# A two-layer FoX and NSA decoder on one Trainium2 core: the end of w_up in 256 columns, weight sums by accumulating transfers, the first output half behind the products, compressed scores by two heads

## The chip, the cores and the metric

The kernel runs on one core of one Trainium2 chip. Its engines are named here as the profile names them: PE is the matrix engine (PEld its weight loads), DVE is VectorE, ACT is ScalarE, POOL is GpSimd, and SP only issues transfers. Each engine works through its own instructions in a fixed order; a transfer is issued by SP, ACT or POOL and then runs by itself. The metric is the time of one execution on the device, in microseconds (us), as the median of several runs.

## The reference

A trunk of two layers on x of 512 tokens by 1024 channels, all in float32, with a final RMSNorm. Per layer:

```python
h = rmsnorm(x, norm_mix)
proj = h @ w_in                      # q, k, v, gates of both mixers
o_a = fox_attention(...)             # 8 heads of 64, softmax(q k / 8 + c_i - c_j), causal
o_c, o_s, o_w = nsa_attention(...)   # 8 heads, 2 key heads: compressed, selected, window
o_n = g[..., 0:1] * o_c + g[..., 1:2] * o_s + g[..., 2:3] * o_w
mixed = sigmoid(gate_a) * (o_a @ w_o_fox) + sigmoid(gate_b) * (o_n @ w_o_nsa)
x = x + mixed @ w_out
h = rmsnorm(x, norm_mlp)
x = x + square(relu(h @ w_up)) @ w_down      # 1024 -> 4096 -> 1024
```

The compressed branch scores each query against 31 compressed keys per key head (blocks of 32 tokens, stride 16); four query heads share a key head. The MLP is the larger half of the work.

## The kernel before

Everything is kept transposed: channels on the 128 partitions, the 512 tokens along the free axis. Every float32 product is made of three reduced-precision products: a value is split into a high part (`h`, a copy to float32r) and a low part (`lo`, the rest), and `h*xh + h*xl + lo*xh` is summed in PSUM (`gemm`, L243 to L245). So each weight block costs one cast on ACT and one subtraction on DVE before PE can use it.

**Order.** The program is written as Python generators that interleave stages by hand, and a tile framework fixes the order of each engine's instructions when the program is built: what comes first in the text has priority, but an instruction whose inputs its plan takes to be ready may be pulled ahead of others. Buffers are named by a tag with a number of copies (`BUFS`); a new tile under a tag waits until an old one's last reader is done.

**Fox heads.** `scores`, `transposes` and `values` run as a three-stage pipeline over 8 heads. `transposes` turns four by four blocks of probabilities in three groups; in the third (`g == 2`) 128 zero columns are set by two memsets (L472, L473), so that in `values` (L491) both the third and the fourth key block multiply 256 columns. `q_pair` makes a query pair: `hilo` splits it into the tile `hl` (two heads of 64 rows, high and low), transfers lay it out as `q2`, and for Fox heads POOL clears two tiles `qx` (L419, L420).

**Compressed scores.** `cmp_probs` (L731) takes, per key head, four query heads, each with `q2` (high and low queries stacked on 128 rows) against `kcz`, a zero-padded key tile (high, then low): 4 x 2 matmuls of 512 columns into one bank.

**MLP.** The first 8 of 32 column blocks of w_up are plain. The other 24 are done in twelve units `g` = 4 to 15 of two blocks, each a fast 2 by 2 scheme with seven products in place of eight (class `Strassen`). `unit` makes the seven products (L1500; each is four steps of a matmul of 512 columns, `h` against high and low tokens at once, and one of 256, `lo` against high), so the sum of the two halves has to be added on DVE afterwards (`halves`, L1560). `A.copy` lines (L1525 to L1535) take sums out of a bank before a later product is added onto it. `act` then squares the positive part and splits it: ACT writes `h` (L1574), POOL the rest (L1575). While a unit runs, the weights of the next are converted (`convert`), and `between` puts in a part of w_down's first six eighths (`down` in `mlp`, L1099).

The last quarter of w_down (four pairs, `g` = 16 to 19) is done in the same scheme with seven products of 256 columns (`Strassen.down`, L1306; each of the four steps is three matmuls). `operands` makes one weight operand at a time in the order of `PARTS` and `LATE`: a cast on ACT (L1263), a subtraction on DVE (L1264). Two of the weight sums are made on DVE: `n2` = -(s1 + a11) in L1259 and `s4` = a12 - n2 in L1261. Another, s1, is made while loading by an accumulating transfer from POOL's queue (L1462, L1471). `combine` makes the sums of the activations: three operations on `tf` (L1273 to L1275), a cast (L1277) and a subtraction (L1278) into `tt`, which has four buffers.

**The end.** In the last layer the first 256 tokens are finished before the last products. `out(x, 0, ...)` makes the norm's factor (`rstd`, L301 to L325), multiplies eight blocks of x by it, half on DVE and half on POOL (L1161), and writes them (L1163); the rest of the products follow, and then `out(x, 1, ...)`. The squares of the second half are summed on POOL (`sumsq`, L287) but for the last block, which goes to the matmul apart.

Of the kernel before, what the change touches and what calls it, by code (L numbers as in the profile page):

```python
# [19 lines left out]
T = 512  # L20
# [123 lines left out]
class Body:  # L144
    def __init__(self, ctx, tc, nc, a):
# [8 lines left out]
                hl=2, r=1, crs=1, zc=4, tt=4, small=1, cc=1, s4=6, big=1, g4=2)  # L154
# [40 lines left out]
    def fetch(self):  # L195

        if self.plan:
# [209 lines left out]
    def q_pair(self, x, fox=False):  # L407

        hl = self.hilo(x, 0.125)
        q2 = self.t("q2", [128, 2, T], F32R)  # L410
        for e in range(2):
            for f in range(2):
                self.nc.sync.dma_start(q2[f * 64:(f + 1) * 64, e].bitcast(F32),
                                         hl[e * 64:(e + 1) * 64, f].bitcast(F32))
        if not fox:
            return q2
        qx = self.two("o2", "qx")
        for e, t in enumerate(qx):
            self.nc.gpsimd.memset(t[64:128].bitcast(F32), 0.0)  # L419
            self.nc.gpsimd.memset(t[64:66].bitcast(F32), 1.0)  # L420
            self.nc.sync.dma_start(t[:64].bitcast(F32), hl[e * 64:(e + 1) * 64, 0].bitcast(F32))
        return q2, qx
# [32 lines left out]
    def transposes(self, u):  # L455
        nc = self.nc
        E = u["E"]
        u["pt"] = []
        for g in range(3):
            ps = self.p("PT")  # L460
            if g < 2:
                todo = [(i, g) for i in range(g, NB)]
            else:
                todo = [(3, 3), (2, 2), (3, 2)]
# [9 lines left out]
            nc.scalar.copy(h[:, o:o + n], ps[:, :n])  # L474
            nc.vector.tensor_sub(lo[:, o:o + n], ps[:, :n], h[:, o:o + n].bitcast(F32))
            u["pt"].append((h, lo))
            yield

    def values(self, u):
        nc = self.nc  # L480
        if u.get("first", True):
            u["O"][0] = self.p("O")
        O = u["O"][0]
        first = u.get("first", True)
        pt = u["pt"]
        last = u.get("last", True)
        todo = [(0, 0, 0, 512), (1, 1, 0, 384), (2, 2, 256, 256), (3, 2, 0, 256)]
        for b, g, o, n in todo:
            v = u["v"](b)
            for f in range(2):  # L490
                nc.tensor.matmul(O[:, T - n:], v, pt[g][f][:, o:o + n],  # L491
                                 start=first and b == 0 and f == 0, stop=last and b == 3 and f == 1)
            yield
        if "after" in u:
            u["after"]()
# [131 lines left out]
    def compress(self, kc, vc, small, l):  # L627
# [83 lines left out]
        nc.scalar.copy(self.kcz[:, :, 0, 96:128], k2)  # L711
        nc.vector.tensor_sub(self.kcz[:, :, 1, 96:128], k2, self.kcz[:, :, 0, 96:128].bitcast(F32))
# [10 lines left out]
    def cmp_probs(self, hk, q2):  # L723
# [4 lines left out]
        for r in range(4):  # L728
            q = q2[2 * hk + r // 2][:, r % 2]
            for f in range(2):  # L730
                nc.tensor.matmul(sc, self.kcz[:, hk, f, 96 - 32 * r:224 - 32 * r], q,  # L731
                                 start=r == 0 and f == 0, stop=r == 3 and f == 1)
# [39 lines left out]
    def setup(self, first):  # L772

        nc, a = self.nc, self.a
        if first:
            self.ident = self.tiny[:, 688:816]
            nc.sync.dma_start(self.ident, a["const"][:, :128])
        t = self.t("long", [128, 2048], name="ct")
        self.ct, self.R = t[:, :N_CONST - 128], t[:, 1024:1536]
        if not first:  # L780
            nc.gpsimd.tensor_copy(self.ct[:, :1], self.acc[0][:, :1])
        nc.sync.dma_start(self.ct, a["const"][:, 128:])
        if first:
# [4 lines left out]
        self.kcz = t[:, 512:1408].rearrange("p (h f n) -> p h f n", h=2, f=2)  # L788
# [71 lines left out]
    def layer(self, l, u):  # L860
# [11 lines left out]
        R, rc = self.rstd(self.acc, ("O", "O"), wait=g, R=self.R)  # L872
        run(g)
# [37 lines left out]
        st = {}  # L911
# [7 lines left out]
        def fox_unit(h):  # L919
            p, e = divmod(h, 2)  # L920
            un = dict(q=lambda: st["qa", p][0][:, e], qx=lambda: st["qa", p][1][e], k=lambda: st["ka", p][e], O=[None],
# [3 lines left out]
            def after():  # L925
                if e == 0:
                    st["oa", p] = self.t("zz", [128, T], name="o")
                self.out_half(un["O"][0], st["oa", p], e)
# [10 lines left out]
        def qproj(p):  # L939
            return proj(12 + p, ("qb", p), lambda ps: self.q_pair(self.roped(ps)))  # L940

        def cmp_gen(hk):
            yield from self.cmp_probs(hk, [st.get(("qb", p)) for p in range(4)])
# [207 lines left out]
    def out(self, x, f, acc, wait, mid=False):  # L1151
# [5 lines left out]
        for k, w in ((0, 2), (6, 1), (2, 2), (7, 1), (4, 1), (5, 1)):  # L1157
            y = self.t("t2", [128, 2, n], name="y")[:, :w]
            for j in range(w):
                pool = k > 5 or f == 0 and j  # L1160
                (nc.gpsimd if pool else nc.vector).tensor_tensor(  # L1161
                    y[:, j], x[k + j][:, f * n:(f + 1) * n], r if f and pool else R, op=OP.mult)
            (nc.scalar if f and k > 5 else nc.sync).dma_start(a["yT"][f, :, k:k + w], y)  # L1163
# [50 lines left out]
class Strassen:  # L1214
# [9 lines left out]
    def __init__(self, body, l, x, gm):  # L1224
# [10 lines left out]
    PARTS = [("a11", 0), ("a12", 0), ("n2", 0), ("a11", 1), ("a12", 1), ("n2", 1), ("a22", 0), ("s3", 0), ("a22", 1),  # L1235
             ("s3", 1)]
# [11 lines left out]
    def operands(self, n):  # L1248
# [3 lines left out]
        for k, g in plan[self.made:self.made + n]:  # L1252
# [4 lines left out]
            src = dict(a11=a11, a12=a12, n2=a11, s4=a12, s1=s1, a22=r2[:, 512:], s3=s3)  # L1257
            if k == "n2":
                nc.vector.scalar_tensor_tensor(a11, s1, -1.0, a11, op0=OP.mult, op1=OP.subtract)  # L1259
            if k == "s4":  # L1260
                nc.vector.tensor_tensor(a12, a12, a11, op=OP.subtract)  # L1261
# [3 lines left out]
            self.ops[k, g] = h, lo  # L1265
            yield

    def combine(self, p):
# [3 lines left out]
        t = b.t("zz", [128, 4, 256], name="tf")  # L1272
        V.tensor_tensor(t[:, 0:3:2], v[:, 0:4:3], v[:, 1:2].to_broadcast([128, 2, 256]), op=OP.subtract)  # L1273
        V.tensor_tensor(t[:, 1], t[:, 0], v[:, 3], op=OP.add)
        V.tensor_tensor(t[:, 3], t[:, 1], v[:, 2], op=OP.subtract)  # L1275
        o = b.t("tt", [128, 4, 2, 256], F32R, name="tt")
# [4 lines left out]
    def down(self, acts):  # L1281
# [10 lines left out]
        def side(k):  # L1292
            if k not in xs:
# [3 lines left out]
                i = dict(s1=0, n2=1, s3=2, a22=3)[k]  # L1297
# [18 lines left out]
        def first(g):  # L1316
# [9 lines left out]
            for h in (g, g + 1):  # L1326
                yield from product("n2", h, m[h])
                V.tensor_tensor(x1[h][:, hi], x1[h][:, hi], m[h], op=OP.add)
            for k, h in (("a22", g), ("s3", g), ("a22", g + 1), ("s3", g + 1)):
                if k == "a22":  # L1330
                    ps = yield from product(k, h)
                    V.tensor_tensor(x2[h][:, lo], x2[h][:, lo], ps, op=OP.subtract)
                else:
                    yield from product(k, h, m[h])
                    v = x2[h].rearrange("p (k c) -> p k c", k=2)
                    V.tensor_tensor(v, v, m[h][:, None, :].to_broadcast([128, 2, 256]), op=OP.subtract)
                    if last:
# [32 lines left out]
        if not last:  # L1370
            b.load_small(l + 1)
            for g in (16, 18):
                run(first(g), second([(k, g + i) for k, i in self.LATE]))
# [6 lines left out]
        b.out(x, 0, acc[0], rest)  # L1380
        run(rest)
        b.out(x, 1, acc[1], iter(()))
# [110 lines left out]

    def product(self, ps, g, i, new):
# [9 lines left out]
    def unit(self, g, D, n, acts):  # L1504
# [11 lines left out]

        def product(i, onto=None):
            ps = b.bank() if onto is None else onto
            self.product(ps, g, i, onto is None)
            return ps  # L1520

        m = product(0)
# [17 lines left out]
        tag = "kd" if g > 13 else "o2"  # L1540
# [72 lines left out]
```

## Time and profile before

| | |
|---|---|
| median of 3 runs | 1534.23 us (1533.68 to 1536.3) |
| profiled execution | 1531.75 us, span 1530.0 us |
| granted PE clock, mean | 0.996 |
| PE busy, DVE busy | 98%, 76% |
| ACT busy, POOL busy | 55%, 13% |

"Busy" of PE is a modelled duration of overlapping matmuls, so 98% does not mean that PE runs at its peak; the spacing from one matmul to the next, as the chain of waits shows it, is the price of one. The views used are the page, the waits (who waited for whom, us in total, times, longest), the chain that ended last (start, us, what), the timeline (start, us, engine, line, operation, tiles, shapes, count; in brackets the idle time before it and what ended it), groups of instructions (count | busy, mean ns | idle before), and a table by window. L12 is line 12 of the kernel.

### The profile page before, as it was taken

Reading aid. Unit: us, or ns where it says so; the run is one execution under the profiler, and the core shown is the slowest. Engines: PE = TensorE matmul, PEld = TensorE weight load, DVE = VectorE, ACT = ScalarE, POOL = GpSimd, SP = SyncE. Lnnn points to the kernel's source line nnn. Section 1 sums busy time; section 2 is a strip of 40 time slices with the busy share of each in tenths; the row PEclk is TensorE's granted clock in tenths of the full one; section 3 lists DMA queues with packets and bytes.
Section 4 is the critical chain, followed back from the end, with each engine's and each line's share of the span. In section 5 each row is a group of like instructions: output and inputs, shape, how many; then the busy total and the mean of one; then the engine's idle time right before and its main releaser. Section 6 shows DMA issues by size and latency. Waiting matters only on the chain.

```text
span 1530.0 us, 21619 instructions
## 1 busy us (share of the span) xinstructions
PE 1503.9 (98%) x7792; PEld 1264.2 (83%) x7792; DVE 1163.8 (76%) x2244; ACT 834.3 (55%) x1578; POOL 201.1 (13%) x200
## 2 busy tenths in 40 slices
PE   9999999999999999998999999999999999999997
PEld 8878888887888888887988788888888888888886
DVE  5678978777488777779846799787674968766796
ACT  6465655554464655556444556555544636555565
POOL 4000000001200222223120000000012002212223
PEclk9999999999999999999999999999999999999998
DMA  8555412137325464546246543321463355554431
GB/s 298 138 161 133 143 56 83 56 98 220 103 92 144 134 161 124 148 136 171 94 146 162 155 120 98 96 69 61 136 184 97 97 158 147 147 147 119 116 97 56
DMA packets 71035, 195.14 MB, mean 128 GB/s; under 512 B 8944, under 2 KB 10352, under 8 KB 70928
## 3 DMA queue, kind: packets, MB, share of 16 engines
q1 hardware_dynamic: 57824, 170.41, 36.1%
q0 software_dynamic: 9216, 16.78, 6.3%
q10 hardware_dynamic: 3888, 6.58, 1.2%
q8 instruction: 61, 1.00, 0.3%
q14 instruction: 46, 0.38, 0.1%
HBM read 149.62 MB, written 4.19 MB: 101 GB/s over the span
## 4 chain that ended last, share of the span: by engine, by line
PE 89%; DVE 6%; ACT 3%; issue 1%; DMA 1%; POOL 0%; DVEq 0%; SPq 0%; ACTq 0%; POOLq 0%
PE ps_mm L243 12%; PE ps_mm L244 12%; PE ps_mm L245 12%; PE ps_S L1500 3%; PE ps_O L1500 3%; PE ps_PT L243 3%; PE ps_PT L244 3%; PE ps_PT L245 3%; PE ps_mm L1500 3%; PE ps_O L618 2%; PE ps_PT L592 2%; PE ps_PT L1500 2%; PE ps_S L567 2%; PE ps_S L243 2%; PE ps_S L245 2%; PE ps_S L244 2%
## 5 line engine op out<-in xcount | busy, mean ns | idle before, releaser
L217 ACT CAST wh<-raw 128x1024 fp32r<-128x1024 f32 (+2 forms) x177 | 181.4, 1027 | 204.7 <-PE ps_mm L244 70.8
L218 DVE TENSOR_TENSOR wl<-raw,wh 128x1024 fp32r<-128x1024 f32 (+2 forms) x177 | 211.7, 1196 | 31.9 <-ACT wh L217 21.3
L243 PE MATMUL ps_mm<-u,wh 128*128 128x512 f32 x512 | 204.1, 399 | 0.0
L245 PE MATMUL ps_mm<-u,wl 128*128 128x512 f32 x512 | 202.0, 395 | 0.0
L244 PE MATMUL ps_mm<-u,wh 128*128 128x512 f32 x512 | 201.9, 394 | 0.0
L1490 DVE TENSOR_TENSOR s<-raw,s 128x512 fp32r<-128x512 f32 x168 | 133.9, 810 | 58.9 <-ACT s L1489 57.4
L1462 POOL DMA_DIRECT2D raw<-raw x32 | 27.9, 871 | 729.1 <-DMA x<-xs 241.7
L243 PE MATMUL ps_mm<-o,wh 128*128 128x512 f32 x284 | 112.2, 396 | 1.7 <-ACT o L508 1.7
L1489 ACT CAST s<-raw 128x512 fp32r<-128x512 f32 x168 | 101.7, 620 | 22.1 <-PE ps_mm L1500 6.0
L245 PEld LDWEIGHTS ps_mm<-u,wl 128*128 128x128 f32 x512 | 96.2, 188 | 21.0 <-issue 0.8
L243 PEld LDWEIGHTS ps_mm<-u,wh 128*128 128x128 f32 x512 | 96.5, 189 | 19.2 <-DVE wl L218 1.5
L245 PE MATMUL ps_mm<-o,wl 128*128 128x512 f32 x284 | 111.7, 393 | 0.0
L244 PE MATMUL ps_mm<-o,wh 128*128 128x512 f32 x284 | 111.3, 392 | 0.0
L244 PEld LDWEIGHTS ps_mm<-u,wh 128*128 128x128 f32 x512 | 96.4, 188 | 16.7
L596 ACT CAST pth<-ps_PT 128x384 fp32r<-128x384 f32 (+1 forms) x96 | 48.9, 512 | 65.3 <-PE ps_PT L592 65.1
L554 DVE CUSTOM_DVE_ANT_0 E<-ps_S,ct 128x384 f32<-128x384 f32 (+3 forms) x112 | 57.4, 515 | 31.7 <-PE ps_S L567 30.4
L555 ACT ACTIVATE E<-E,tiny 128x384 f32<-128x384 f32 (+3 forms) x112 | 65.6, 586 | 21.2 <-DVE tiny L554 20.8
L597 DVE TENSOR_TENSOR ptl<-ps_PT,pth 128x384 fp32r<-128x384 f32 (+1 forms) x96 | 56.8, 599 | 13.8 <-ACT pth L596 12.4
L243 PEld LDWEIGHTS ps_mm<-o,wh 128*128 128x128 f32 x284 | 53.3, 188 | 13.1 <-ACT o L508 2.6
L245 PEld LDWEIGHTS ps_mm<-o,wl 128*128 128x128 f32 x284 | 53.4, 188 | 11.7
L244 PEld LDWEIGHTS ps_mm<-o,wh 128*128 128x128 f32 x284 | 53.4, 188 | 10.8 <-DVE o L509 0.9
L243 PE MATMUL ps_PT<-o,wh 128*128 128x512 f32 x156 | 61.4, 394 | 0.0
(406 smaller groups left out, 3747.7 us busy)
## 6 DMA issues: line engine op xcount, KB each, us to landing
raw<-wb SPq DMA_DIRECT2D x64, 512.0 KB
raw<-wup SPq DMA_DIRECT2D x64, 512.0 KB
raw<-wd SPq DMA_DIRECT2D x48, 512.0 KB
raw<-raw POOLq DMA_DIRECT2D x64, 256.0 KB, 4.1
w<-w SPq DMA_DIRECT2D x32, 256.0 KB
kda<-hla SPq DMA_DIRECT2D x32, 256.0 KB
q2a<-hla SPq DMA_DIRECT2D x64, 128.0 KB
raw<-wo SPq DMA_DIRECT2D x16, 512.0 KB
```

The costliest lines, as they stand in the source:

```text
L217: nc.scalar.copy(h[:, :n], raw[:, :n])
L218: nc.vector.tensor_tensor(lo[:, :n], raw[:, :n], h[:, :n].bitcast(F32), op=OP.subtract)
L243: mm(ps, h[:, c], xh, start=start and i == 0, stop=False)
L244: mm(ps, h[:, c], xl, start=False, stop=False)
L245: mm(ps, lo[:, c], xh, start=False, stop=stop and i == ks - 1)
L554: nc.vector.tensor_tensor_reduce(e, ps, self.mask[:, T - n:], -1.0, BIG, OP.add, OP.min, mx)
L555: nc.scalar.activation(e, e, AF.Exp, bias=mx, scale=-1.0, accum_out=un["sm"][:, i:i + 1])
L596: nc.scalar.copy(h[:, e, :n], ps[:, :n])
L597: nc.vector.tensor_sub(lo[:, e, :n], ps[:, :n], h[:, e, :n].bitcast(F32))
L1489: nc.scalar.copy(h, src)
L1490: nc.vector.tensor_tensor(lo, src, h.bitcast(F32), op=OP.subtract)
L1500: mm = lambda o, w, x, **kw: self.nc.tensor.matmul(o, w, x, skip_group_check=True, **kw)
```

## The change

It has these parts:

- `Strassen.unit` takes, for the last three pairs (`g` > 12, `slim`), `narrow` in place of `product`: three matmuls of 256 columns per step into half a bank, as w_down's products do. The sum of high and low is made in PSUM; `halves` is not called, the copies are of 256 columns, and the activations are made in the tile `z` itself.
- `operands` makes the sums s2 = a11 + s1 and s4 = a12 + s2 by accumulating transfers from POOL's queue, each issued when the operand that it overwrites has been converted. Signs in `combine` follow (s2 in place of n2), `tf` gets a tag with one buffer, and `tt`'s four tiles come from the tags `tt`, `kd` and twice `long`. In `first`, s3 and then a22 are summed onto the same bank, each taken off one half of x.
- `out` gives back a function that writes; for the first half it is called after the last products. The sums of squares of blocks 5 and 6 of the second half are made on DVE.
- `cmp_probs` reads `hl` (two heads on 128 rows) against a block-diagonal `kcz`: two pairs of heads, three matmuls each (high-high, low queries, low keys).
- Fox: no zero columns in the third group; the fourth key block multiplies 128 columns. In the second layer a one-column copy of `rc` into each `qx` stands before its memsets.

```diff
-                hl=2, r=1, crs=1, zc=4, tt=4, small=1, cc=1, s4=6, big=1, g4=2)
+                hl=2, r=1, crs=1, zc=4, tt=1, tf=1, small=1, cc=1, s4=6, big=1, g4=2)
...
+            if self.late:
+                self.nc.gpsimd.tensor_copy(t[64:128, :1], self.rc[64:128, :1])
             self.nc.gpsimd.memset(t[64:128].bitcast(F32), 0.0)
...
-            o = 0
-            if g == 2:
-                o = 128
-                nc.vector.memset(h[:, :128].bitcast(F32), 0.0)
-                nc.vector.memset(lo[:, :128].bitcast(F32), 0.0)
...
-        todo = [(0, 0, 0, 512), (1, 1, 0, 384), (2, 2, 256, 256), (3, 2, 0, 256)]
+        for b, g, o, n in ((0, 0, 0, 512), (1, 1, 0, 384), (2, 2, 0, 256), (3, 2, 256, 128)):
...
-        for r in range(4):
-            q = q2[2 * hk + r // 2][:, r % 2]
-            for f in range(2):
-                nc.tensor.matmul(sc, self.kcz[:, hk, f, 96 - 32 * r:224 - 32 * r], q,
-                                 start=r == 0 and f == 0, stop=r == 3 and f == 1)
+        for p in range(2):
+            k = self.kcz[:, hk, :, 64 - 64 * p:192 - 64 * p]
+            for i, (f, e) in enumerate(((0, 0), (0, 1), (1, 0))):
+                nc.tensor.matmul(sc, k[:, f], hl[2 * hk + p][:, e], start=p == 0 and i == 0, stop=p == 1 and i == 2)
...
-    PARTS = [("a11", 0), ("a12", 0), ("n2", 0), ("a11", 1), ("a12", 1), ("n2", 1), ("a22", 0), ("s3", 0), ("a22", 1),
-             ("s3", 1)]
+    PARTS = [("a11", 0), ("a12", 0), ("a11", 1), ("a12", 1), ("s2", 0), ("s2", 1), ("s3", 0), ("s3", 1),
+             ("a22", 0), ("a22", 1)]
...
-            if k == "n2":
-                nc.vector.scalar_tensor_tensor(a11, s1, -1.0, a11, op0=OP.mult, op1=OP.subtract)
-            if k == "s4":
-                nc.vector.tensor_tensor(a12, a12, a11, op=OP.subtract)
...
+            if k == "a11":
+                nc.gpsimd.dma_start(a11, s1, accum_op=OP.add)
+            if k == "s2":
+                nc.gpsimd.dma_start(a12, a11, accum_op=OP.add)
...
-        t = b.t("zz", [128, 4, 256], name="tf")
+        t = b.t("tf", [128, 4, 256], name="tf")
...
-        o = b.t("tt", [128, 4, 2, 256], F32R, name="tt")
+        o = b.t(("tt", "kd", "long", "long")[p], [128, 4, 2, 256], F32R, name="tt")
...
-            acc[f] = b.sumsq(xm, acc[f], m == 7 and ("sum", "apart")[f])
+            acc[f] = b.sumsq(xm, acc[f], ("sum", "apart")[f] if m == 7 else f and m > 4)
...
-        b.out(x, 0, acc[0], rest)
+        write = b.out(x, 0, acc[0], rest)
         run(rest)
-        b.out(x, 1, acc[1], iter(()))
+        write()
+        b.out(x, 1, acc[1], iter(()))()
...
+    def narrow(self, ps, g, i, new):
+        h, lo = self.ops[g][i]
+        mm = lambda o, *z, **kw: self.nc.tensor.matmul(o, *z, skip_group_check=True, **kw)
+        for p in range(4):
+            c = slice(p * 128, (p + 1) * 128)
+            x = self.xs[i][p]
+            mm(ps, h[:, c], x[:, 0], start=new and p == 0, stop=False)
+            mm(ps, h[:, c], x[:, 1], start=False, stop=False)
+            mm(ps, lo[:, c], x[:, 0], start=False, stop=p == 3)
...
+        if slim:
+            m = product(0)
+            z = b.t("zc", [128, 2, 512], name="z")
+            lo, hi = slice(0, 256), slice(256, 512)
+            A.copy(z[:, 1, lo], m)
...
+            product(4, m)
+            v = z[:, 0].rearrange("p (k c) -> p k c", k=2)
+            V.tensor_tensor(v, v, m[:, None, :].to_broadcast([128, 2, 256]), op=OP.add)
+            self.act(z[:, 0], acts, tag)
...
+            product(6, p5)
+            V.tensor_tensor(z[:, 1, hi], z[:, 1, hi], p5, op=OP.subtract)
+            self.c.append(z)
+            self.act(z[:, 1], acts, tag)
```

More of the change, by code (lines that the diff above doesn't have):

```diff
@@ L195, in fetch @@
     def fetch(self):
-        if self.plan:
+        if self.plan and self.plan[0] is not None:
             src, n, *tag = self.plan.popleft()
@@ L1149, in mlp, with out @@
         return S.down(acts[24:])
-    def out(self, x, f, acc, wait, mid=False):
+    def out(self, x, f, acc, wait):
         nc, a = self.nc, self.a
@@ L1326, in first @@
             for h in (g, g + 1):
-                yield from product("n2", h, m[h])
+                yield from product("s2", h, m[h])
                 V.tensor_tensor(x1[h][:, hi], x1[h][:, hi], m[h], op=OP.add)
[L1329 to L1333, printed above, removed]
+            for k, s in (("s3", hi), ("a22", lo)):
+                for h in (g, g + 1):
                     yield from product(k, h, m[h])
-                    v = x2[h].rearrange("p (k c) -> p k c", k=2)
-                    V.tensor_tensor(v, v, m[h][:, None, :].to_broadcast([128, 2, 256]), op=OP.subtract)
-                    if last:
+                    V.tensor_tensor(x2[h][:, s], x2[h][:, s], m[h], op=OP.subtract)
+                    if last and k == "a22":
                         done(h, 0)
```

107 lines of the change are left out of this document (65 added, 42 removed).

## The prediction

> **What bounds the kernel now.** I read the page first (its span and busy shares), then the waits of the matrix engine alone in the two stretches that the change edits most (end of w_up and w_down of each layer), then the timeline there for the engine named. The page:
>
> ```profile
> span 1530.0 us, 21619 instructions
> PE 1503.9 (98%) x7792; PEld 1264.2 (83%) x7792; DVE 1163.8 (76%) x2244; ACT 834.3 (55%) x1578; POOL 201.1 (13%) x200
> ```
>
> PE is the bound: nothing is won unless PE gets less work or waits less. All sums below are made against this execution, 1531.75 us with a span of 1530.0; it stands 2.5 us under the median of the runs, 1534.23. The waits of PE, layer 0 (660 to 770 us), then layer 1 (1420 to 1530 us); columns: who waited, for whom, us in total, times, longest.
>
> ```profile
> PE ps_mm L1306 <- POOL ohl L1575: 2.2, 1, 2.2
> PE ps_PT L1306 <- ACT tt L1277: 2.0, 1, 2.0
> PE ps_PT L1306 <- DVE tt L1278: 0.7, 1, 0.7
> ...
> PE ps_mm L1306 <- ACT ohl L1574: 0.4, 1, 0.4
> ```
> ```profile
> PE ps_PT L301 <- POOL acc L287: 2.6, 1, 2.6
> PE ps_O L318 <- DVE tiny L312: 2.1, 2, 1.3
> PE ps_O L243 <- DVE y L1548: 1.1, 1, 1.1
> PE ps_PT L1306 <- POOL ohl L1575: 1.0, 1, 1.0
> PE ps_mm L1306 <- DVE tt L1278: 0.6, 1, 0.6
> PE ps_mm L1306 <- ACT tt L1277: 0.3, 1, 0.3
> ```
>
> So PE's few long waits sit exactly at the w_up/w_down seam: 5.3 us in layer 0 (2.2 + 0.4 for the last activation's low part `ohl`, 2.0 + 0.7 for the combined activations `tt`), 3.0 us in layer 1, and 4.7 us in the tail. Why are `ohl` and `tt` late? VectorE is full there (window 690 to 730, columns PE, PEld, DVE, ACT, POOL busy):
>
> ```profile
> 690.00:730.00 40.00, 34.32 (x204) 29.77 (x203) 38.11 (x57) 23.48 (x38) 13.49 (x17) 0.98 0.55 158
> ```
> ```profile
> 711.30 0.68 DVE L1548 TENSOR_TENSOR y<-y,ps_S 128x512 f32<-128x512 f32 x1
> ...
> 716.54 0.61 ACT L1574 CAST ohl<-z 128x512 fp32r<-128x512 f32 x1
> ...
> 717.09 0.91 POOL L1471 DMA_DIRECT2D raw<-raw  x1
> ...
> 717.62 0.52 POOL L420 MEMSET qx<- 2x512 f32 x1
> ...
> 718.23 1.56 POOL L1575 TENSOR_TENSOR ohl<-z,ohl 128x512 fp32r<-128x512 f32 x1
> ```
>
> The high part is written at 717.15 (716.54 + 0.61), but GpSimd first ends a transfer's issue and a `qx` memset that belongs to the next layer's attention, pulled ahead by the planner, and starts the low part 1.1 us late. Behind VectorE the whole chain had begun late already.
>
> **The change part by part.**
>
> *Matrix work.* The prices are spacings on PE, from the chain of waits (start, us, what):
>
> ```profile
> 701.08 1.42 PE ps_PT L1500 x8
> ...
> 733.19 1.44 PE ps_PT L1306 x12
> ```
> ```profile
> 182.62 1.87 PE ps_S L731 x8
> ...
> 195.05 0.33 PE ps_PT L592 x3
> ```
>
> Compressed scores: per layer and key head 8 matmuls of 512 columns become 6; 8 go in all, at 1.87/8 = 0.234 us: -1.9. PE is dense around them, so all of it counts. They now read `hl`, which has two buffers; both are held until the scores, and the next user of `hl` is the projection after them, so nothing queues: 0.
>
> w_up in 256 columns: a product of four steps was 8 matmuls (512 and 256 columns in turn), 1.42 us; now it is 12 of 256 columns, the very form of L1306, 1.44 us, and elsewhere L1500's eight show 1.40 to 1.41 as well. 3 pairs x 7 products x 2 layers = 42 products x 0.02 to 0.04: +0.8 to +1.7. I take +1.3.
>
> Fox values: 2 matmuls per head, 32 in all, go from 256 columns (zero-padded) to 128. At 256 columns one costs 1.44/12 = 0.120. No matmul of this type under 256 columns is in the trace. Nearest below: the 128-column transposes, 0.33/3 = 0.11 each, which gives -0.3. Nearest above: full-precision 128-column matmuls, which leave two records each, 0.22 apart (L817 to L816):
>
> ```profile
> 52.06 0.38 PE L817 MATMUL ps_S<-ct,tiny 128*8 128x128 f32 x2
> 52.28 0.38 PE L816 MATMUL ps_S<-tiny 128*8 128x128 f32 x2
> ```
>
> That gives 32 x 0.10 = +3.2. I take 0: the transposes share with the new matmul that they are one record with a 128-column weight load. [...] The two memsets per head that go (VectorE, fox stage) are hidden: PE shows no long wait there; 0.
>
> *VectorE, ScalarE and GpSimd at the seam.* What leaves VectorE in the window 690 to 730, by its groups:
>
> ```profile
> L1278 DVE TENSOR_TENSOR tt<-tf,tt 128x1024 fp32r<-128x1024 f32 x4 | 4.8, 1218 | 0.0
> ...
> L1560 DVE TENSOR_TENSOR z<-z 128x512 f32<-128x512 f32 x2 | 1.4, 684 | 0.0
> L1560 DVE TENSOR_TENSOR z<-y 128x512 f32<-128x512 f32 x2 | 1.4, 682 | 0.0
> L1259 DVE SCALAR_TENSOR_TENSOR raw<-raw 128x512 f32<-128x512 f32 x2 | 1.4, 678 | 0.0
> L1261 DVE TENSOR_TENSOR raw<-raw 128x512 f32<-128x512 f32 x2 | 1.3, 686 | 0.0
> ```
>
> The additions of the two halves (L1560) go, 2.8; the weight sums L1259 and L1261 become transfers, 2.7; and the four subtractions of L1544/L1548 shrink from 0.68 to the 0.41 that 256 columns take (L1347 below), 1.1. That is 6.6 of 38.1 us, and 31.5 of 40 is left. In the last unit the chain from the last product to `ohl` loses 0.68 (halves) and 0.27 (narrower subtraction), besides the queue ahead of it. The `qx` memsets of layer 1 now wait for that layer's `rc` and so can't stand before `ohl`: 0.5 us and more each. They move to the start of layer 1, where GpSimd waits most of the time; each pays one tiny copy there: 0.
>
> So the `ohl` waits go (2.2 + 0.4), and of the `tt` waits in layer 0 (2.7) I let 2.0 go and 0.7 stay: -4.6. In layer 1: 1.1 (a product's bank held by L1548) and 1.0 (`ohl`) go, of the `tt` waits 0.9 I let 0.6 go: -2.7. The other order of the products (s3 and a22 on one bank) changes no PE count; one subtraction of 512 columns becomes 256: 0.
>
> *Eight more accumulating transfers per layer* (a11 += s1, a12 += a11 for four pairs), each an issue on GpSimd and a landing. They replace 0.68 us on VectorE by this:
>
> ```profile
> raw<-raw POOLq DMA_DIRECT2D x64, 256.0 KB, 4.1
> ```
> ```profile
> DMA to landing us min/median/max: 3.0/4.7/10.6
> ```
>
> An issue is 0.91 (L1471 above), which queues the `ohl` subtractions of L1575 behind it, and its own wait, for a11's conversion on VectorE, holds GpSimd too. From a11's conversion to s2's there are at least three products, 3 x 1.44 = 4.3 us; issue and median landing are 5.0 to 5.6. So ScalarE, in order, may stand about 1.3 us before casting s2, and behind it stand the last unit's activations. Their slack: two w_down products of 512 columns and two of w_up's last halves lie between, over 5 us. I take 0; bounds: 0, and 6.3 more us per late landing (10.6 against 4.3).
>
> *`combine` with one `tf` buffer.* Each of four pairs is now serial: three small VectorE operations (0.68, 0.41, 0.41), ScalarE's cast, VectorE's subtraction 1.2 (L1278).
>
> ```profile
> 726.27 2.00 ACT L1277 CAST tt<-tf 128x1024 fp32r<-128x1024 f32 x2 [4.75 <-DVE tf L1275]
> ```
>
> That is 1.5 + 1.0 + 1.2 = 3.7 us a pair. The first pair's inputs are there three units before the last pair's; if three pairs fall behind the last unit, 11 us must fit in the two w_down products (12 matmuls of 0.234 each, 2.8) and four products of `first`, 2 x 2.8 + 4 x 1.44 = 11.4. It just fits, and this is why I left 0.7 standing.
>
> *The tail.*
>
> ```profile
> 1514.25 3.39 DVE L1161 TENSOR_TENSOR y<-x,R 128x256 f32<-128x256 f32 x4
> ...
> 1515.85 0.88 PE L1306 MATMUL ps_S<-ohl,d 128*128 128x256 f32 x6
> ...
> 1517.89 0.41 DVE L1347 TENSOR_TENSOR x<-x,ps_S 128x256 f32<-128x256 f32 x1
> ...
> 1518.55 0.73 POOL L287 TENSOR_TENSOR acc<-sq,acc 128x256 f32<-128x256 f32 x1 [0.33 <-POOL acc L287]
> ...
> 1520.42 0.16 DVE L304 TENSOR_SCALAR tiny<-ps_PT 128x2 f32<-128x2 f32 x1 [2.13 <-PE ps_PT L301]
> ```
>
> The last product ends at 1516.73, but its addition starts at 1517.89, behind the first half's four output multiplies, and the sum of squares then waits for GpSimd until 1519.28. With the output written after the products the addition can start at 1516.9 (1.0 us earlier), and with the sum on VectorE (0.42) the squares' matmuls at about 1517.8 in place of 1519.3. But the four multiplies are still VectorE's work, 0.85 each beside GpSimd's four, 0.42 alone:
>
> ```profile
> L1161 DVE TENSOR_TENSOR y<-x,ps_mm 128x256 f32<-128x256 f32 x6 | 2.1, 416 | 2.2 <-PE ps_mm L318 2.2
> ```
>
> Behind the last addition they end between 1519.0 and 1520.7, L304 after them. Gain 1.4 by the first, a loss of 0.3 by the second. I take 1.4, as GpSimd has done its own by then. [...] The first half's transfers move later by some 2 us and are through before the second half's: 0.
>
> Sum: -1.9 + 1.3 + 0 - 4.6 - 2.7 + 0 - 1.4 = -9.3. 1531.75 - 9.3 = 1522.5, and on the scale of the median 1524.9.
>
> **The rivals.** *A: the gain at the seam is given back to `combine`.* One `tf` buffer and borrowed `tt` buffers make the pairs serial; if the planner puts them last, as it did before (`tt` subtractions up to 728), PE waits for the later pairs as before and some more. Then the `tt` waits stay whole (2.0 and 0.6 back) and one more serial pair, 3.7, is paid in one layer: -9.3 + 6.3 = -3.0, 1531.2 on the median's scale. For it: VectorE stays at 31.5 of 40. Against it: the first pair can go three units earlier.
>
> *B: the 128-column values run at the full-precision pace.* +3.2: 1528.1. For it: no row shows a matmul of this type under 256 columns. Against: one record, as in the transposes, is the likelier form. [...]
>
> *C, the other side: accumulating transfers land late.* If each of the 16 lands at the worst of L1462's (10.6) in place of the median, ScalarE stands 6.3 us before s2 or s4, less about 5 of slack: 1.3 us of PE for each, 16 x 1.3 = 21, so 1545.7. It decides from 0.6 us lost per transfer on. Against it: 4.1 us median over 64. [...]
>
> **How the numbers follow.** Forecast (1519 to 1528 on the median's scale) 0.5; B 0.13, of A 0.17 about half within 0.2%; C or any like stall of a shifted plan 0.2. 0.2% is 3.1 us, about what a measurement of this kernel can tell from none. Faster: 0.5 + 0.13 + half of A = 0.72; same 0.08; slower 0.2. Range: from all `tt` waits gone, -0.3 and a full tail (-12: 1522, less 4 for other short waits of PE at the seam, 1518) up to A and the mildest of C, 1537.
>
> **What would show it.** L731's group with 24 in place of 32 matmuls; the products of the last three pairs at 12 x 0.12; L491 at 128 columns spaced 0.11 (B: a spacing or record pair of 0.22); PE's waits for `ohl` gone and for `tt` under 1 us a layer (A: over 3); no L1259/L1261 on VectorE and 80 accumulating transfers landing near 4 us (C: ScalarE waiting on a landing before `d`); L304 of the second half 1.4 us nearer the last product. Wrong would make me: a new wait on PE in the last three units, or a plan that moves work elsewhere.

## The result and the profile after

The changed kernel takes 1543.43 us (median of 6 runs, 1539.35 to 1544.21) against 1533.15 us for the kernel before (6 runs). The ratio is 1.0062, with a 95% interval of 1.0047 to 1.0077: slower by 0.6%, where I had forecast 1524.9 and "faster". The profiled execution took 1543.98 us, 12.2 us more than the profiled one of before. Its page:

```profile
span 1541.9 us, 22037 instructions
PE 1506.9 (98%) x7952; PEld 1274.8 (83%) x7952; DVE 1149.8 (75%) x2188; ACT 835.3 (54%) x1580; POOL 214.0 (14%) x222
...
raw<-raw POOLq DMA_DIRECT2D x80, 256.0 KB, 4.4
```

The totals hide the cause. VectorE has 14 us less to do, and the accumulating transfers are 80 with a median landing of 4.4 us, as the prediction assumed. PE's waits at the seam tell more: layer 0 (660 to 770 us) and, in the second fence, layer 1 (1420 to 1540 us).

```profile
PE ps_PT L1302 <- DVE x L1318: 1.5, 1, 1.5
PE ps_PT L1302 <- ACT tt L1273: 1.4, 1, 1.4
PE ps_PT L1302 <- POOL ohl L1619: 1.2, 1, 1.2
PE ps_PT L1302 <- ACT ohl L1618: 1.1, 1, 1.1
PE ps_mm L1302 <- POOL ohl L1619: 0.9, 1, 0.9
```
```profile
PE ps_PT L243 <- DVE z L1555: 6.0, 1, 6.0
...
PE ps_S L1302 <- DVE x L1336: 1.5, 1, 1.5
```

The waits for `ohl`, which the change was to remove, are still there in layer 0, and layer 1 has a new one of 6.0 us for VectorE's `z`. VectorE isn't full any more: from 690 to 730 us it is busy for 29.24 of 40 us (third of the busy times; 38.11 in the kernel before).

```profile
690.00:730.00 40.00, 34.90 (x236) 32.10 (x235) 29.24 (x40) 22.15 (x41) 13.72 (x13) 0.96 0.67 171
```

So who holds it up? ScalarE's waits (690 to 760 us, then 1455 to 1530 us) name a transfer:

```profile
ACT d L1255 <- DMA raw<-raw: 9.5, 3, 5.9
```
```profile
ACT d L1255 <- DMA raw<-raw: 11.2, 2, 7.5
```

The timeline of layer 1 gives the order (start, us, engine, line, idle time before and its releaser). L1259 is the first weight sum (a11 += s1), L1261 the second (a12 += a11), L1255 the cast of a weight part; the one at 1475.19 is pair 17's s2:

```profile
1463.75 0.89 POOL L1259 DMA_DIRECT2D raw<-raw  x1 [1.56 <-DVE d L1256]
...
1467.69 0.88 POOL L1261 DMA_DIRECT2D raw<-raw  x1 [1.71 <-DVE d L1256]
...
1468.32 1.14 POOL L1259 DMA_DIRECT2D raw<-raw  x1
...
1469.35 1.60 PE L1493 MATMUL ps_O<-b,s 128*128 128x256 f32 x12
...
1475.19 0.62 ACT L1255 CAST d<-raw 128x512 fp32r<-128x512 f32 x1 [7.50 <-DMA raw<-raw]
1475.71 0.62 ACT L1616 ACTIVATE z<-z 128x512 f32<-128x512 f32 x1
...
1476.44 0.42 DVE L1555 TENSOR_TENSOR z<-ps_S,z 128x256 f32<-128x256 f32 x1
...
1476.92 0.79 PE L243 MATMUL ps_PT<-o,wh 128*128 128x512 f32 x1 [5.97 <-DVE z L1555]
1477.51 0.63 PE L244 MATMUL ps_PT<-o,wh 128*128 128x512 f32 x1
1477.94 0.63 PE L245 MATMUL ps_PT<-o,wl 128*128 128x512 f32 x1
```

Pair 17's first sum is issued at 1468.32, behind pair 16's second sum, and is in SBUF only at 1475.19, when ScalarE begins the cast. For 7.5 us ScalarE stands before that cast, and behind it in its queue stands the last unit's activation (L1616); VectorE waits for ScalarE (L1256, then L1555), and PE has nothing after 1470.95. By the trace, pair 16's second sum lands at 1471.85 and pair 17's first 3.3 us later; 3.3 us is also the fastest landing of these sums. Layer 0 is alike: the same cast waits 5.9 us, and the cast of `ohl` (L1618) stands behind it. The last two lines show a second price: 512-column matmuls are 0.43 us apart, where they are 0.23 apart in dense stretches. The granted clock was 0.57 from 1477 to 1482 us (the number before the last two):

```profile
1477.00:1482.00 5.00, 5.00 (x13) 3.95 (x14) 3.49 (x5) 4.14 (x7) 3.72 (x4) 0.57 0.57 107
```

To see where the 12 us lie, I divided each profiled span at the end of the last product of w_down in either layer, as the timelines give them (us):

| kernel | to the end of layer 0 | layer 1 | tail | span |
|---|---|---|---|---|
| before | 762.7 | 754.1 | 13.2 | 1530.0 |
| after | 767.6 | 763.1 | 11.2 | 1541.9 |
| before, sums by transfers (e3) | 771.6 | 763.1 | 11.3 | 1546.0 |
| after, first sum by transfer only (e11) | 763.2 | 758.1 | 11.5 | 1532.8 |
| after, sums on VectorE (e1) | 758.1 | 754.9 | 11.5 | 1524.5 |
| before, 256 columns only (e14) | 755.2 | 753.7 | 10.7 | 1519.6 |
| e15, below | 756.6 | 750.5 | 11.7 | 1518.7 |

Layer 0 loses 4.9 us, layer 1 9.1 (before rounding), and the tail gains 2.0.

### The profile page after: what moved, and what is told of

Read it like the earlier page. It is cut to its first block, busy times and chain, and to the rows that moved or that the text cites. A ratio compares the mean times of both kernels' runs of the same rounds, so it can differ in the third digit from the quotient of the medians.

```text
span 1541.9 us, 22037 instructions
## 1 busy us (share of the span) xinstructions
PE 1506.9 (98%) x7952; PEld 1274.8 (83%) x7952; DVE 1149.8 (75%) x2188; ACT 835.3 (54%) x1580; POOL 214.0 (14%) x222
## 5 line engine op out<-in xcount | busy, mean ns | idle before, releaser
L1486 DVE TENSOR_TENSOR s<-raw,s 128x512 fp32r<-128x512 f32 x168 | 138.4, 836 | 54.6 <-ACT s L1485 53.6
L586 DVE TENSOR_TENSOR ptl<-ps_PT,pth 128x384 fp32r<-128x384 f32 (+1 forms) x96 | 56.8, 599 | 13.7 <-ACT pth L585 12.3
L245 PEld LDWEIGHTS ps_mm<-o,wl 128*128 128x128 f32 x284 | 53.4, 188 | 11.7
```

What stands on the lines that cost most here:

```text
L245: mm(ps, lo[:, c], xh, start=False, stop=stop and i == ks - 1)
L586: nc.vector.tensor_sub(lo[:, e, :n], ps[:, :n], h[:, e, :n].bitcast(F32))
L1486: nc.vector.tensor_tensor(lo, src, h.bitcast(F32), op=OP.subtract)
```

## The experiments

Theory T: the loss comes from the weight sums as transfers. Rival R: it comes from something else (narrow products, buffers, the new order of the products). Each was timed beside the kernel before on the same chip; the ratios are to that.

**e1, the sums on VectorE again.** Everything else of the change stays.

```diff
+            if k == "s2":
+                nc.vector.tensor_tensor(a11, s1, a11, op=OP.add)
+            if k == "s4":
+                nc.vector.tensor_tensor(a12, a12, a11, op=OP.add)
...
-            if k == "a11":
-                nc.gpsimd.dma_start(a11, s1, accum_op=OP.add)
-            if k == "s2":
-                nc.gpsimd.dma_start(a12, a11, accum_op=OP.add)
```

> The changed kernel with w_down's weight sums s2 and s4 made by additions on VectorE again, and no added transfer; all other parts of the change stay. Theory T (the added transfers: ScalarE stands before the cast of s2 until the sum has landed, 5.9 us in layer 0 and 7.5 us in layer 1, and the last unit's activations stand behind it): PE's 6.0 us wait for z (L1555) and the waits for ohl behind the casts go, 1531 to 1536 us against 1543. Rival R (the narrow products, the single tf buffer and the plan that they shift): 1540 us or more, with PE's long waits still there.

Measured: 1526.45 us, ratio 0.9965 [0.9951, 0.9978]. That is 17 us under the changed kernel by the medians, and 15 by the ratios to the runs of the kernel before beside each: more than the whole loss, and T's range was too cautious. VectorE's eight additions a layer, which the transfers had saved, cost less here than the transfers. PE's waits for `tt` in layer 0, then in layer 1:

```profile
PE ps_PT L1302 <- ACT tt L1273: 2.5, 1, 2.5
PE ps_PT L1302 <- DVE tt L1274: 0.6, 1, 0.6
```
```profile
PE ps_mm L1302 <- ACT tt L1273: 1.3, 1, 1.3
```

**e2, the same transfers with time to land.** The two a11 come first, s3 is converted before s2, and the second sum is issued behind a22.

```diff
-    PARTS = [("a11", 0), ("a12", 0), ("a11", 1), ("a12", 1), ("s2", 0), ("s2", 1), ("s3", 0), ("s3", 1),
+    PARTS = [("a11", 0), ("a11", 1), ("a12", 0), ("a12", 1), ("s3", 0), ("s3", 1), ("s2", 0), ("s2", 1),
...
-            if k == "s2":
+            if k == "a22":
                 nc.gpsimd.dma_start(a12, a11, accum_op=OP.add)
```

> The changed kernel with the transfers, but with the operands made in the order a11, a11, a12, a12, s3, s3, s2, s2, a22, a22, and the second sum's transfer issued after a22: nothing on GpSimd's queue stands between the two a11 sums, and each has two more conversions' time to land. T: ScalarE's waits for a landing before d go under 1 us each, 1530 to 1536 us. If the transfers cost by their issue or their traffic and not by the wait: above 1538. R: 1540 or more.

Measured: 1528.37 us, ratio 0.9975 [0.9966, 0.9983], under T's range. No cast waits for a transfer here. The landings (us; in each fence the first sum's line, then the second's; first the changed kernel, then this one) show what changed:

```profile
DMA to landing us min/median/max: 3.3/3.7/7.9
...
DMA to landing us min/median/max: 3.3/4.5/5.5
```
```profile
DMA to landing us min/median/max: 3.3/3.6/4.9
...
DMA to landing us min/median/max: 3.3/4.7/8.8
```

The slow landings have moved from the first sum, which s2 waits for, to the second, which is needed last. All 16 transfers and their issues are still there, and the kernel is 1.9 us over e1, timed on the same chip. So the loss is in the waits, and at most some 2 us of it in issues or traffic.

**e3, the transfers alone on the kernel before.** Its edit is the diff's `PARTS`, the two transfers, the signs and the new order of w_down's products, nothing else.

> The kernel before with only the weight sums by transfers (operands, their order, the signs in combine and the order of s3 and a22 as in the change; wide products, four buffers). T: ScalarE stands for the landings here too, 5 to 10 us over the kernel before, 1538 to 1543. R: within 2 us of the kernel before.

Measured: 1547.04 us, ratio 1.0097 [1.0083, 1.0111]: +15 us, above T's 5 to 10. PE's longest wait in either layer:

```profile
PE ps_PT L1306 <- ACT ohl L1570: 7.3, 1, 7.3
```
```profile
PE ps_O L243 <- DVE y L1544: 9.0, 1, 9.0
```

e1 keeps the new order of the products and is fast, so the order isn't it: these transfers cost some 15 us with and without the rest of the change.

**e11 and e12, one sum at a time**, to part the landing from the queue. T and R in the two forecasts are new: both lie within the first T, T now being the queue and R the landing itself. e11 leaves the first sum a transfer, e12 the second; the other goes to VectorE as in e1.

> The changed kernel with the second weight sum (a12 += a11) taken back to VectorE; the first (a11 += s1) stays an accumulating transfer. Theory T (the loss comes from the order on GpSimd's queue: pair 16's second sum stands ahead of pair 17's first sum and waits there for s2's conversion): with no second sum in the queue the first one is issued as soon as a11 is converted, ScalarE stands less than 2 us before s2, PE has no wait of 5 us at the seam, 1526 to 1530 us. Rival R (a landing of 4 to 8 us is too long for the room between a11's conversion and s2's, whatever stands in the queue): ScalarE still waits over 4 us for the landing and PE over 4 us behind it, 1536 to 1543 us.

> The changed kernel with the first weight sum (a11 += s1) taken back to VectorE; the second (a12 += a11) stays an accumulating transfer. s4 is used last of all, so its landing has some 20 us of room. T and R both expect no wait for a landing at the seam: 1526 to 1529 us. A third reading, that accumulating transfers in this stretch slow the weight loads or the other engines whatever waits for them, expects part of the loss to stay: 1532 us or more.

e11 measured 1534.91 us (1.0013 [1.0004, 1.0021]), between the two theories; e12 1523.8 us (0.9937 [0.9924, 0.9949]). The timeline of e11 in layer 1 (here L1261 is the first sum, L1257 the cast):

```profile
1461.23 0.88 POOL L1261 DMA_DIRECT2D raw<-raw  x1 [1.57 <-DVE d L1258]
...
1465.92 0.62 ACT L1257 CAST d<-raw 128x512 fp32r<-128x512 f32 x1 [4.52 <-DMA raw<-raw]
...
1467.68 0.80 PE L243 MATMUL ps_PT<-o,wh 128*128 128x512 f32 x1 [3.06 <-DVE z L1555]
```

No other sum is under way (pair 16's landed at 1460.76), the landing takes 4.7 us, the longest of this run (median 3.3), and ScalarE still waits 4.5 of it: R's part is true. In the changed kernel the same wait was 7.5. There pair 17's first sum is issued 4.6 us behind pair 16's (1468.32 - 1463.75), here 3.8 behind (from the same two issues of this run), and its landing takes 6.9 us behind another transfer instead of 4.7: 0.8 + 2.2 = 3.0 us more, which is T's part. In time the two weigh alike: of the way from 1.0062 to e1's 0.9965, half (to 1.0013) goes with the second sum out of the queue. The second sum alone is harmless: no cast waits for it in e12. The 2.5 us by which e12 lies under e7 (below; both sums on VectorE, same chip) are within what the intervals can tell. With half the transfers still there, e12 also speaks against a third reading, that the transfers themselves slow the stretch.

**e14, the 256 columns alone**, with the buffers that they need.

```diff
-                hl=2, r=1, crs=1, zc=4, tt=4, small=1, cc=1, s4=6, big=1, g4=2)
+                hl=2, r=1, crs=1, zc=4, tt=1, tf=1, small=1, cc=1, s4=6, big=1, g4=2)
...
+        slim = g > 12
...
-            ps = b.bank() if onto is None else onto
-            self.product(ps, g, i, onto is None)
+            ps = (b.bank()[:, :256] if slim else b.bank()) if onto is None else onto
+            (self.narrow if slim else self.product)(ps, g, i, onto is None)
```

> The kernel before with the last three pairs of w_up in 256 columns alone, and the buffers of the combined activations that this needs (one tf, tt borrowed); attention, weight sums, order of the products and tail as before. My step of the seam (waits for ohl and tt gone, -7.3, and +1.3 for the products themselves) expects about -5, since 3.9 of the 6.6 us that I took from VectorE go here: 1526 to 1528 us. Rival A (one tf buffer makes the pairs serial and PE waits for tt instead) expects the ohl waits gone and 2 to 3 us of tt waits a layer: 1530 to 1532 us.

Measured: 1521.83 us, ratio 0.9933 [0.992, 0.9947], 10.0 us under the kernel before. One part of the change brings all of its gain, and more than I had asked of the whole. PE's waits in layer 0 and then in layer 1:

```profile
PE ps_PT L1306 <- ACT tt L1277: 1.0, 1, 1.0
```
```profile
PE ps_S L1306 <- DVE x L1344: 1.5, 1, 1.5
PE ps_mm L1306 <- ACT tt L1277: 1.3, 1, 1.3
PE ps_PT L301 <- POOL acc L287: 0.4, 1, 0.4
```

No wait for `ohl` is left, and 1.0 us remains of the 5.3 in layer 0. By the table, layer 0 gains 7.5 and the tail 2.5, layer 1 only 0.3 (before rounding).

**e4, the attention parts alone** (compressed scores by two heads, 128-column Fox values).

> The kernel before with only the parts in the attention: compressed scores by two heads and Fox values without zero columns. Both theories: 8 matmuls of 0.234 us less, and 0.6 us less in the value products by the sum of PE's spacings in the two traces (23.9 against 23.3 us), so -2.5 us. If a shifted plan alone moves the time by several us: anywhere from -5 to +3.

Measured: 1532.68 us, ratio 0.9998 [0.9989, 1.0007]. PE has less work and is early: the first product of w_down's seam starts at 711.45 against 712.63. Then it is lost. The windows 700 to 718 and 718 to 736, first of the kernel before, then of this one (PE, PEld, DVE, ACT, POOL busy, granted clock, DMA share, GB/s):

```profile
700.00:718.00 18.00, 16.86 (x97) 14.19 (x95) 17.80 (x27) 14.76 (x25) 10.39 (x15) 1.00 0.76 237
718.00:736.00 18.00, 13.47 (x97) 13.06 (x98) 16.85 (x28) 5.53 (x8) 1.70 (x2) 0.91 0.25 55
```
```profile
700.00:718.00 18.00, 15.63 (x90) 13.09 (x88) 17.80 (x28) 13.61 (x23) 10.04 (x16) 1.00 0.82 241
718.00:736.00 18.00, 14.65 (x85) 14.24 (x86) 14.47 (x23) 5.41 (x8) 0.61 (x1) 0.72 0.21 52
```

Until 718 VectorE is as full in both (17.80 of 18), and the same `ohl` and `tt` waits end as before: the product that starts at 731.84 in the kernel before starts at 731.92 here. Then the lower clock shows: 18 x (0.91 - 0.72) = 3.4 us more of it in the second window, part of them while PE waits anyway, and the product of 734.71 starts at 736.22 here, 1.5 us late.

**e7 and e10, the tail**, both with the sums on VectorE. e7 writes the first half's output as the kernel before does; e10 keeps the write behind the products and puts all its multiplies on GpSimd and all of the second half's sums of squares on VectorE.

```diff
-                    pool = k > 5 or f == 0 and j
+                    pool = k > 5 or f == 0
...
-            acc[f] = b.sumsq(xm, acc[f], ("sum", "apart")[f] if m == 7 else f and m > 4)
+            acc[f] = b.sumsq(xm, acc[f], ("sum", "apart")[f] if m == 7 else f)
```

> The changed kernel with both weight sums on VectorE, and the first half's output written as before (in program text ahead of the last products, its sums of squares on GpSimd). If the edit of the tail is worth what I forecast (1.4 us), this takes 1.4 us more than the same kernel with the new tail (1526.45): 1527.9. If the planner's order makes both tails alike (in both, four multiplies of 0.9 us stand before the last additions), the difference is only the sum of squares (1.1 us less waiting) against the new 1.5 us wait for the addition: 1526.0 to 1527.0.

> The changed kernel with both weight sums on VectorE, and all eight output multiplies of the first half on GpSimd, all sums of squares of the second half on VectorE. If PE's 1.5 us wait for the addition in the tail comes from the four multiplies ahead of it on VectorE, that wait goes and the time is 1.0 to 1.5 us under 1526.45: 1525.0 to 1525.5. If GpSimd's eight multiplies (0.7 us each, 5.6 us) slow VectorE's additions or end too late for the second half's, it is 1526 to 1528.

e7 measured 1526.32 us (0.9955 [0.9941, 0.9969]), the same as e1, and e10 1524.24 (0.9941 [0.9929, 0.9954]). The tail of the changed kernel, then of e10:

```profile
1525.08 3.51 DVE L1155 TENSOR_TENSOR y<-x,R 128x256 f32<-128x256 f32 x4
...
1528.51 0.41 DVE L1336 TENSOR_TENSOR x<-x,ps_S 128x256 f32<-128x256 f32 x1
...
1529.07 0.95 PE L1302 MATMUL ps_S<-o,d 128*128 128x256 f32 x6 [1.50 <-DVE x L1336]
```
```profile
1506.97 6.13 POOL L1155 TENSOR_TENSOR y<-x,R 128x256 f32<-128x256 f32 x8 [6.52 <-ACT R L329]
...
1507.96 0.42 DVE L1336 TENSOR_TENSOR x<-x,ps_S 128x256 f32<-128x256 f32 x1
```

"Behind the products" stands in the program text only. In the order that was run, the four multiplies still come ahead of the last additions and hold a bank of PE for 1.5 us. With no multiply on VectorE the wait is gone, and e10 is 2.1 us under e7. It moves the sums of squares as well; no run parts the two.

**e8, the qx memsets free again** (`self.late` always false; otherwise e1).

> The changed kernel with both weight sums on VectorE, and the memsets of qx free to be pulled ahead, as before. If holding them behind the layer's rc is worth what I said, layer 0's ohl wait comes back in part and this takes 0.5 to 1.1 us more than 1526.45: 1527.0 to 1527.6. If not, it is within 0.5 us of 1526.45.

Measured: 1527.12 us, ratio 0.9964 [0.9952, 0.9977] against e1's 0.9965: no difference that can be told, and PE has no wait for `ohl` in layer 0.

**e13 and e15, the parts that pay together.** e13 is e12 with e10's tail. e15 is the kernel before with the 256 columns, the attention parts and e10's tail, but the old sums and the old order of w_down's products.

> The changed kernel with the first weight sum on VectorE, the second as a transfer, and the first half's eight output multiplies on GpSimd. The first measured 1523.8 and the second 2.2 us under its own base; if the two gains lie in different places (seam and tail) they add: 1521.5 to 1522.5 us. If the gain of the second sum's transfer was the planner's luck at another place, 1523.5 to 1525.

> The kernel before with w_up's last three pairs in 256 columns and their buffers (1521.8 alone), the compressed scores by two heads and the 128-column Fox values, and the first half's output behind the products with all its multiplies on GpSimd; the weight sums and the order of w_down's products as before. It differs from the kernel with both sums on VectorE and the output on GpSimd (1524.2) in the order of w_down's products, in the sums' signs, and in the qx memsets. If the matrix work saved in attention (1.2 us) and the tail's wait (1.5 us) now reach the end: 1518.5 to 1520. If the edits beside the 256 columns bring nothing of their own, as attention alone did: 1521.5 to 1522.5. If they cost time: 1524 or more.

e13 measured 1522.15 us (0.9934 [0.9921, 0.9946]), the two gains nearly adding up. e15 measured 1520.62 us (0.9926 [0.9913, 0.994]), the fastest of all, between its first two forecasts, though within its interval of e14.

## Why the prediction was wrong

**The step that failed: the eight more accumulating transfers a layer, costed at 0.** I had let ScalarE stand 1.3 us before s2, with over 5 us of slack behind it. Both halves were wrong. First, I counted three products (4.3 us) between a11's conversion and s2's. But conversions run ahead of the products. In e11 the sum is issued at 1461.23, and ScalarE is ready for the cast at 1461.40 (1465.92 - 4.52), while the first of these products starts at 1474.73. There is no product between, so nearly the whole landing is a wait. Second, the slack in layer 1 is 1.5 us, not over 5: ScalarE's 7.50 became PE's 5.97 in the changed kernel, and 4.52 became 3.06 in e11. In layer 0 it was longer: 3.9 us of ScalarE's wait in e11 leave PE no wait for `ohl`, 5.9 us in the changed kernel leave 3.2. To this came a queue that I had named but priced only by its issue: behind another transfer the landing took 6.9 to 7.9 us. So rival C was right in mechanism (ScalarE before s2, the last unit behind it), and not in its sum: that 1545.7 lay near the 1543.43 that was measured is luck, since not all 16 transfers land late, as C had it. Two, pair 17's first sum in each layer, make the longest waits: 5.9 of the 9.5 us that ScalarE waits for these transfers in layer 0, and 7.5 of 11.2 in layer 1.

**The matrix work: right, but for the Fox values.** The compressed scores are priced as forecast: six matmuls take 1.36 us from their first start to the next matmul's (184.63 to 185.99), where eight took 1.87, and over the four groups it is -2.0 (forecast -1.9). The narrow products start 1.44 us apart, as forecast. The Fox values came out cheaper than my lower bound (starts, us; PEld are the weight loads):

```profile
878.89 0.19 PEld L481 LDWEIGHTS ps_O<-pth,vf 128*128 128x128 f32 x1
879.12 0.19 PEld L481 LDWEIGHTS ps_O<-ptl,vf 128*128 128x128 f32 x1
879.23 0.19 PEld L243 LDWEIGHTS ps_mm<-u,wh 128*128 128x128 f32 x1
```
```profile
879.12 0.22 PE L481 MATMUL ps_O<-pth,vf 128*128 128x128 f32 x1
879.18 0.27 PE L481 MATMUL ps_O<-ptl,vf 128*128 128x128 f32 x1
879.29 0.45 PE L243 MATMUL ps_mm<-u,wh 128*128 128x512 f32 x1
```

The two take 0.06 + 0.11 = 0.17 us, against 2 x 0.12: up to 16 heads x 0.07 = -1.1. Rival B is false. So is my 0, taken because transposes and new matmuls alike have a 128-column weight load: here the first one's load (878.89) runs beside the matmul ahead (L444, 878.89 to 879.12), and only the second's is seen, 0.11 us from its start to the next load's.

What the sum missed was that less work ahead of the seam was not less time. In e4 the 1.2 us that these savings bring to the seam at 711 us are gone by 731.9, since VectorE, busy for 17.80 of 18 us ahead of them in both, sets when the waits end, and the longer half clock takes 1.4 us more. Whether they count once the seam is relieved is not shown: e15 lies 1.2 us under e14, within what the intervals can tell, it has e10's tail besides, and its first product starts later (713.27 against 712.08).

**The seam, -7.3 and +1.3: right and too low in layer 0, not parted in layer 1.** e14 alone brings -10.0 with 3.9 of VectorE's 6.6 us. In layer 0 the `ohl` waits go as said, and 7.5 us are won where I had 4.6, less some 0.7 for the products. I had left out that the half-clock stretch behind those waits goes with them (3.4 us long in the kernel before, at most 1.7 us of loss by my estimate; the granted clock of 718 to 736 us is 0.91 there and 1.00 in e14). In layer 1 the `ohl` wait goes too, but 1.5 us of PE's wait for `x` (L1344) come in ahead of the last product. The tail, which e14 doesn't edit, is 2.5 us shorter: its wait for `acc` is 0.4 us in place of 2.6. So part of the 10.0 is a gain that I didn't forecast, and no run shows why it comes. The `qx` memsets, which I had held responsible in part, make no difference in e8.

**`combine`: between the forecast and rival A.** I let 0.7 us of `tt` waits stay in layer 0 and 0.3 in layer 1. With everything but the transfers (e1) they are 3.1 and 1.3 us, as large as before or larger, which is A's claim; in e14, with the same buffers, 1.0 and 1.3. But the other gains weren't given back: A expected 1531.2, and e1 took 1526.45.

**The tail, -1.4: nothing.** The changed kernel's tail is 2.0 us shorter, but PE waits 1.5 us more ahead of it, e14 has both without the edit, and e7 shows that the edit is worth nothing; I took the program text for the order. Nor does a run show the four multiplies at 0.42 us: that was the mean of six with an operand from `ps_mm`, beside two of GpSimd's (1523.36 to 1524.77 us in the kernel before). The four took 3.51 us in the changed kernel, still beside GpSimd's four.

**The clock** was in no step of mine. From 660 us on, the half-clock stretches at the seams last 13.7 us in the changed kernel against 3.4 in the kernel before: (13.7 - 3.4) / 2 = 5.1 us. But for the first 2.45 us of the stretch in layer 1 (1474.47 to 1476.92) PE was waiting anyway, so it is at most 3.9 of the 12 us.

What stays open: the planner put pair 16's second sum ahead of pair 17's first, and why it did (its cost of a landing, or its due times) wasn't tried. Nor was a kernel with the transfers in which that order alone is turned round, or one with wide products and one `tf`. The first 490 us are 1.3 us longer in the changed kernel; no run isolates that.

## What to carry to other kernels

Price an operation that moves to a transfer by its landing (here 3.3 to 7.9 us for the first sums) against the work that the *consumer's in-order engine* has left before it, as the trace has it, and not against the products that lie between in the program; then ask what stands behind the waiting instruction. On GpSimd's queue here, a transfer that waited 1.71 us for a late result held up the one behind it (pair 17's first sum: issued 0.8 us later behind pair 16's than in e11, and 6.9 us to its landing in place of 4.7), so put there only results that are needed last (here the second sum). And measure the parts of a bundle one by one: here one part in five held the gain (10.0 us), and another lost half as much again (some 15 us).

## What the hardware showed

A wait of PE cost more than its length in some places of these runs, and not in others. Ten of the 14 profiled runs have stretches of half clock (granted clock 0.50) ahead of the tail. They last 3.413 us or a multiple, and in each run they and the tail's stretch start whole multiples of 3.413 us apart (in the changed kernel at 726.95, 733.78 and 1474.47 us, 2 and 217 such steps). So I divided each of the 14 runs into windows of that length, in phase with these starts (with the tail's where there is no other), and added up PE's idle time in each, from 30 to 1500 us: from one matmul's start to the next, less its columns' time at full clock, 0.233 us for 512. All 16 full-clock windows with 2.15 to 3.41 us idle were followed by half clock, and none with up to 2.06 us was: in the kernel before 2.6 us were idle ahead of the stretch at 728.40 us, and in the changed kernel 2.31, 2.45 and 3.41 ahead of its three, with at most 1.9 in any other full-clock window of the two. With 0.213 to 0.240 us for 512 columns both bounds move by some 0.1 us at most, and the two groups stay apart. That is a count over these runs; no run shows what sets the clock. By it, a wait of some 2.5 us was followed by half clock where it lay in one window, and not where an edge split it. e12 and then e13, alike at this place, with the same wait and different clocks (window 712 to 736; the granted clock stands before the last two numbers):

```profile
PE ps_PT L1302 <- ACT tt L1273: 2.4, 1, 2.4
...
712.00:736.00 24.00, 21.48 (x159) 20.73 (x158) 20.91 (x36) 10.23 (x16) 6.23 (x7) 0.93 0.52 136
```
```profile
PE ps_PT L1302 <- ACT tt L1273: 2.4, 1, 2.4
...
712.00:736.00 24.00, 21.52 (x170) 20.53 (x169) 21.84 (x38) 11.67 (x18) 5.63 (x6) 1.00 0.56 140
```

In e12 one window holds 2.64 us of idle time; in e13 two neighbours hold 2.06 and 1.24. Short waits added up as well: in the changed kernel's layer 0 several of up to 1.5 us made 2.31 and 2.45 in a window. My estimate of the price is up to 1.7 us for each stretch of 3.413 us (half of it), as far as PE has work there.
